# DeltaNet stage of a decoder block: channel weights split in two halves, z copied out of PSUM by ScalarE, the output's turn one chunk later

## The chip, the cores and the metric

One core of a Trainium2 chip. The metric is the device time of the kernel in microseconds, the median of several executions. One execution was also recorded by the hardware profiler; all rows below come from that one.

## What is computed

A decoder block on 1024 tokens of width 1024: an attention branch, a gated DeltaNet branch, a mixture of experts and a per-layer embedding. The change touches the way in which channels of one large input projection are computed, and the DeltaNet branch, which is this (8 heads of width 128):

```python
proj = h @ w_in
qkv_b = silu(causal_short_conv(qkv_b, conv_w))           # q, k, v of each head
beta = sigmoid(beta_b); g = -exp(a_log) * softplus(alpha_b + dt_bias)
a_mat = tril_strict((k * beta) @ k.T * decay)            # inside each chunk
t_mat = inverse(eye + a_mat)                             # unit lower triangular
u, w = t_mat @ (v * beta), t_mat @ (k * beta * exp(gcum))
# over the chunks:
v_new = u - w @ state
o     = (q * exp(gcum)) @ state + attn_intra @ v_new
state = state * exp(g_last) + k_tail.T @ v_new
# at the end:
o_b = rms_norm(o) * silu(z)
```

## The kernel before

Matrix products of the projection are made in fp32r with both operands split: a weight `w` becomes `whi` (a copy rounded to fp32r, by ScalarE, `wsplit` L182) and `wlo = w - whi` (VectorE, L183), and each product is three matmuls (`mm3`, L37 to L39). Engines are called PE (TensorE), ACT (ScalarE), DVE (VectorE), POOL (GpSimd) and SP (which here only issues DMAs).

`channels` (L201) is the projection, one job for 128 channels. A job loads a raw weight of 128x8x128 by a DMA from SP (`wraw`, L173), splits it, and does two halves of 512 tokens, 24 matmuls of 128x512 each, into a PSUM tile `mm` (2 buffers); after each half the job's `done` takes the tile out. The weight of the next job is loaded and split when half 0 is through. There are 2 buffers for `wraw` and 3 for `whi` and `wlo`, so the raw weight of the load after next can be fetched only when both instructions of the present split have read theirs. 42 loads feed the DeltaNet stage (32 of the heads, 10 of gates), 6 more run at the end of the attention stage.

`delta_net` runs the 8 heads as a software pipeline over this feed: one head is one period of 32 feed steps, 4 jobs (k, q, v, z). What a head does between the feed's matmuls is placed by the table `P`: `rows` fetches a row of decays `D` (L711), `decay` makes `eg` and `D` of it (ACT L719 to L724), `job_k`, `job_q`, `job_v` end in a short convolution (ACT L632 and L634, DVE L636 three times, ACT tanh L637, DVE L638), `job_z` in ACT tanh L669 and DVE L671, which reads PSUM, then a DMA `zT` to DRAM (L672). The matrix `nat` (L741) is written to DRAM as `dA` by four DMAs (L751) and comes back spread over 128 partitions as `M` by one DMA (`M<-dA`, L753). `solve` then works on DVE alone: a memset of M's diagonal (L757), and 31 pairs of L764 and L766 with growing width; its result goes through `dT` to `um`. `inverse` joins 32-blocks to the full triangle by small matmuls `px`, `py`, `pyt` (L845 to L868), with copies by ACT and DVE (`xz` L848/L849, `tm` L856, `um` L857/L858, `x` L864).

`scan` is the recurrence over 8 chunks: matmul `pks` (L911), DVE `vb` (L913), matmul `pvn` (L917), ACT `vn` (L920), matmul `po` (L922), matmul `pds` (L930), DVE `S` (L936). After every 4 chunks `out` normalizes: sums `so` (L888, L889), `ro` by DVE L110 and a power on POOL (L111), DVE L891, then ACT `on` (L894, four copies). `turn` transposes `on` on PE (`pot`, L899), multiplies by z on DVE (L900) and stores (`obT`, L902, SP). `late` says how many chunks of the next scan steps lie between `out` and `turn`.

The instruction order on each engine is fixed before the run: a list scheduler goes over the program in the order in which it is written and puts each instruction on its engine by its model of when it is ready, with a priority for the recurrence (`hp`). Each engine, SP too, then works through its list in order and stops at the first instruction whose inputs or buffers are not ready. So an edit that makes more or other instructions can shift others that it does not mention.

Of the kernel before, what the change touches and what calls it, by code (L numbers as in the profile page):

```python
# [11 lines left out]
AF = mybir.ActivationFunctionType  # L12
ALU = mybir.AluOpType
# [18 lines left out]
def r32(ap):  # L32
    return ap.bitcast(F32)


def mm3(nc, out, lh, ll, rh, rl, start, stop):
    nc.tensor.matmul(out, lh, rh, start=start, stop=False)  # L37
    nc.tensor.matmul(out, lh, rl, start=False, stop=False)  # L38
    nc.tensor.matmul(out, ll, rh, start=False, stop=stop)  # L39
# [67 lines left out]
def rstd_pow(k, out, ss, n, eps=EPS):  # L107
    nc = k.nc
    w = out.free_size() if callable(getattr(out, "free_size", None)) else out.shape[-1]
    nc.vector.tensor_scalar(out, ss, 1.0 / n, eps, op0=ALU.mult, op1=ALU.add)  # L110
    return nc.gpsimd.tensor_tensor(out, out, k.mhalf[:, :out.shape[-1]], op=ALU.pow)  # L111
# [57 lines left out]
def wraw(k, srcs, shape=(8, 128), eng=None):  # L169

    raw = k.wpool.tile([128, *shape], F32, name="wraw", tag="wraw", bufs=k.wbufs[0])
    for sl, s in srcs:
        (eng or k.nc.sync).dma_start(raw[sl], s)  # L173
    return raw


def wsplit(k, raw):
    nc = k.nc
    shape = raw.shape[1:]
    hi = k.wpool.tile([128, *shape], F32R, name="whi", tag="whi", bufs=k.wbufs[1])  # L180
    lo = k.wpool.tile([128, *shape], F32R, name="wlo", tag="wlo", bufs=k.wbufs[1])
    nc.scalar.activation(hi, raw, AF.Copy)  # L182
    nc.vector.tensor_tensor(lo, raw, r32(hi), op=ALU.subtract)  # L183
    return hi, lo


def wload(k, srcs, shape=(8, 128), eng=None):
    return wsplit(k, wraw(k, srcs, shape, eng))


def wcols(w, *cols):

    v = w.rearrange("(c p) n -> p c n", p=128)
    out, o = [], 0
    for c0, n in cols:
        out.append(((slice(None), slice(None), slice(o, o + n)), v[:, :, c0:c0 + n]))
        o += n
    return out


def channels(k, jobs):  # L201


    def load(i):
        return wload(k, wcols(k.I["w_in"][0], (jobs[i][0], 128)))

    w = load(0)
    for i, (_, done) in enumerate(jobs):
        for half in range(2):
            p = k.ps_mm.tile([128, 512], F32, name="mm", tag="mm")  # L210
            s = slice(half * 512, half * 512 + 512)
            for c in range(C):
                mm3(k.nc, p, w[0][:, c, :], w[1][:, c, :], k.hh[:, c, s], k.hl[:, c, s], c == 0, c == C - 1)
                if c == C - 1:
                    done(half, p)
                    if half == 0 and i + 1 < len(jobs):
                        then = load(i + 1)
                if c % 2:
                    yield
        w = then if i + 1 < len(jobs) else None  # L220
# [378 lines left out]
def half4(hf):  # L599
    return slice(4 * hf, 4 * hf + 4)  # L600


def cols(x):
    return lambda c: x[:, c * 128:c * 128 + 128]


P = dict(hp=65, every=2, late=(1, 3), tk0=1, tk1=4, rows=0, de0=4, de1=5, kb0=8, kk0=10, kb1=10, kk1=13, solve=15,
         tq0=14, kq0=15, tq1=20, kq1=22, tv0=22, tv1=24, tails=24, turned=37, after=43)


class Head:
# [51 lines left out]
    def job_z(self):  # L663

        k, nc, h = self.k, self.k.nc, self.h

        def done(half, p):
            th = k.thp.tile([128, 512], F32, name="th", bufs=2)
            nc.scalar.activation(th, p, AF.Tanh, scale=0.5)  # L669
            z = k.st.tile([128, 512], F32, name="acc", bufs=2)  # L670
            nc.vector.scalar_tensor_tensor(z, th, 1.0, p, op0=ALU.add, op1=ALU.mult)  # L671
            nc.sync.dma_start(k.zT[h * 128:h * 128 + 128, 512 * half:512 * half + 512], z)  # L672
        return O_QB + 3072 + 128 * h, done

# [148 lines left out]
    def before(self):  # L823
# [8 lines left out]
        for n, g in f.items():  # L832
            slots.setdefault(P[n], []).append(g)
        return slots
# [37 lines left out]
    def scan(self):  # L872

        k, nc, dn, h = self.k, self.k.nc, self.k.dn, self.h
        um = k.um[h % 2]
        hp = lambda: k.tc.high_priority(offset=P["hp"]) if P["hp"] else ExitStack()
        S = None
        late = []

        def out(hf, po):  # L880
            z2 = dn.tile([128, 512], F32, name="z2", bufs=2)
            t4 = slice(512 * hf, 512 * hf + 512)
            nc.sync.dma_start(z2, k.zT[h * 128:h * 128 + 128, t4])
            c4 = half4(hf)
            so = dn.tile([128, 4], F32, name="so", bufs=2)
            self.sumsq(po, so)
            ro = dn.tile([128, 4], F32, name="ro", bufs=2)
            nc.vector.tensor_tensor(so, so, self.rq[:, c4], op=ALU.mult)  # L888
            nc.vector.tensor_tensor(so, so, self.rq[:, c4], op=ALU.mult)  # L889
            rstd_pow(k, ro, so, 128.0)  # L890
            nc.vector.tensor_tensor(ro, ro, self.rq[:, c4], op=ALU.mult)  # L891
            on = dn.tile([128, 4, 128], F32, name="on")
            for i in range(4):
                nc.scalar.activation(on[:, i, :], po[:, i, :], AF.Copy, scale=ro[:, i:i + 1])  # L894

            def turn():
                pt = self.ptile("pot")
                for i in range(4):
                    nc.tensor.transpose(pt[:, i, :], on[:, i, :], k.ident)  # L899
                nc.vector.scalar_tensor_tensor(z2, pt.rearrange("p a b -> p (a b)"), k.dng, z2, op0=ALU.mult,  # L900
                                               op1=ALU.mult)
                nc.sync.dma_start(k.obT[h * 128:h * 128 + 128, t4], z2)  # L902
            late.extend([None] * P["late"][hf] + [turn])

        for c in range(8):
            i = c % 4
            if i == 0:
                po = k.ps_o.tile([128, 4, 128], F32, name="po", tag="o")
            if S is not None:
                ps = k.ps_v.tile([128, 128], F32, name="pks", tag="v")  # L910
                nc.tensor.matmul(ps, cols(self.k2)(c), S, start=True, stop=True)  # L911
                with hp():
                    nc.vector.scalar_tensor_tensor(self.vb[:, c, :], ps, self.co[:, 1, c:c + 1], self.vb[:, c, :],  # L913
                                                   op0=ALU.mult, op1=ALU.add)
# [24 lines left out]
            if i == 3:  # L939
                out(c // 4, po)  # L940
# [472 lines left out]
def expert_split(k, raw):  # L1413
    k.wpool, k.wbufs = k.wgu
    gu = [wsplit(k, r) for r in raw[:4]]
    k.wpool, k.wbufs = k.wdn
    return gu, [wsplit(k, r) for r in raw[4:]]
# [284 lines left out]
def tile_kernel(ctx, tc, I, out):  # L1702
# [25 lines left out]
    with ExitStack() as e0:  # L1728
        with ExitStack() as e1:
# [36 lines left out]
            for i, _ in enumerate(feed):  # L1766
                if i % P["every"] == 0:
                    next(more, None)
# [113 lines left out]
```

## Time and profile before

| | |
|---|---|
| time, median of 3 executions | 2051.33 us (2045.94 to 2053.91) |
| profiled execution | 2063.92 us, span 2062.2 us |
| PE busy | 1962.6 us (95% of the span) |
| PE weight loads | 1672.1 us |
| DVE busy | 1161.1 us (56%) |
| ACT busy | 968.1 us (47%) |
| POOL busy | 195.4 us (9%) |
| mean granted clock of PE | 0.987 |

A busy share is an average over stages: the DeltaNet stage lies from about 580 to 1370 us, its steady heads from 836 to 1240 us with a period of 72 us. An engine whose idle time is named with a releaser was waiting for that instruction or DMA.

### The profile page before, as it was taken

The numbers are of one execution on the slowest core, as the hardware profiler recorded it, in microseconds if no ns is written. First come the engines' busy times: TensorE is split into PE (matmuls) and PEld (weight loads), VectorE is DVE, ScalarE is ACT, GpSimd is POOL, SyncE is SP. The second block draws the span as 40 slices with busy tenths as digits, with TensorE's granted clock in tenths as the row PEclk, the third lists the DMA queues.
The fourth block names the chain that finished last, engine by engine and source line by source line (L and its number), as shares of the span: only waits on it lengthen the run. The fifth ranks groups of instructions, "written<-read, shape, count | busy, mean of one in ns | idle before, by whom it ended". The sixth has DMA issues, their size and how long they took to land.

```text
span 2062.2 us, 35105 instructions
## 1 busy us (share of the span) xinstructions
PE 1962.6 (95%) x13402; PEld 1672.1 (81%) x13402; DVE 1161.1 (56%) x2940; ACT 968.1 (47%) x2573; POOL 195.4 (9%) x196
## 2 busy tenths in 40 slices
PE   7999999999999989999999999979999889999998
PEld 7999999989987777777777777858978767777698
DVE  7253435473422678778877872355474645555655
ACT  6344445444443644565456452232433345555643
POOL 0000000000000001010000100000021244431100
PEclk9999999999999999999999999989999899999999
DMA  4102131242233222232222223585465377776742
GB/s 160 54 28 78 53 105 52 81 138 74 66 110 111 58 67 59 65 85 62 79 76 74 68 68 101 145 246 192 145 204 184 125 238 253 231 246 229 244 157 91
DMA packets 249353, 252.53 MB, mean 122 GB/s; under 512 B 62453, under 2 KB 207142, under 8 KB 248922
## 3 DMA queue, kind: packets, MB, share of 16 engines
q1 hardware_dynamic: 234280, 224.88, 35.8%
q0 software_dynamic: 11776, 24.18, 3.4%
q8 instruction: 107, 1.75, 0.3%
q10 hardware_dynamic: 3122, 1.16, 0.2%
q14 instruction: 68, 0.56, 0.1%
HBM read 202.34 MB, written 64.59 MB: 129 GB/s over the span
## 4 chain that ended last, share of the span: by engine, by line
PE 63%; DVE 14%; DMA 12%; issue 7%; ACT 2%; POOL 1%; SPq 1%; ACTq 0%; DVEq 0%; POOLq 0%
PE mm L37 13%; PE mm L38 13%; PE mm L39 12%; DMA M<-dA 4%; DVE prod L764 3%; DVE tu L766 3%; DMA wraw<-in_w_expert_down_dram 2%; PE gp L37 2%; DVE acc L636 2%; PE gp L39 2%; PE gp L38 1%; PE sc L447 1%; PE pv L475 1%; PE gu L37 1%; PE gu L38 1%
## 5 line engine op out<-in xcount | busy, mean ns | idle before, releaser
L183 DVE TENSOR_TENSOR wlo<-wraw,whi 128x1024 fp32r<-128x1024 f32 x228 | 274.9, 1223 | 213.2 <-ACT whi L182 211.3
L37 PE MATMUL mm<-whi,hTh 128*128 128x256 f32 x1152 | 336.1, 292 | 5.9 <-ACT sqa L406 3.5
L37 PE MATMUL mm<-hTh,whi 128*128 128x512 f32 x768 | 327.0, 426 | 14.7 <-ACT th L962 10.3
L38 PE MATMUL mm<-wlo,hTh 128*128 128x256 f32 x1152 | 327.8, 285 | 0.0
L39 PE MATMUL mm<-whi,hTl 128*128 128x256 f32 x1152 | 327.7, 284 | 0.0
L182 ACT ACTIVATE whi<-wraw 128x1024 fp32r<-128x1024 f32 x228 | 236.0, 1057 | 194.2 <-PE mm L38 113.9
L39 PE MATMUL mm<-hTh,wlo 128*128 128x512 f32 x768 | 304.8, 397 | 0.0
L38 PE MATMUL mm<-hTl,whi 128*128 128x512 f32 x768 | 303.8, 396 | 0.0
L37 PEld LDWEIGHTS mm<-whi,hTh 128*128 128x128 f32 x1152 | 221.8, 193 | 18.0 <-issue 7.3
L38 PEld LDWEIGHTS mm<-wlo,hTh 128*128 128x128 f32 x1152 | 222.1, 193 | 0.8 <-DVE wlo L183 0.7
L39 PEld LDWEIGHTS mm<-whi,hTl 128*128 128x128 f32 x1152 | 221.8, 193 | 0.2 <-DVE rsqx L119 0.2
L37 PEld LDWEIGHTS mm<-hTh,whi 128*128 128x128 f32 x768 | 146.3, 191 | 40.8 <-ACT th L962 10.7
L39 PEld LDWEIGHTS mm<-hTh,wlo 128*128 128x128 f32 x768 | 145.2, 189 | 32.9
L38 PEld LDWEIGHTS mm<-hTl,whi 128*128 128x128 f32 x768 | 146.4, 191 | 22.4
L454 ACT ACTIVATE sm<-sm,nm 128x128 f32<-128x128 f32 (+1 forms) x192 | 84.3, 440 | 87.5 <-DVE nm L452 87.0
L403 ACT ACTIVATE qraw<-mm 128x256 f32<-128x256 f32 x128 | 48.4, 378 | 148.2 <-PE mm L39 148.0
L407 DVE TENSOR_REDUCE ss<-sqa 128x4 f32<-128x256 f32 x96 | 40.1, 418 | 133.0 <-ACT sqa L406 132.9
L636 DVE SCALAR_TENSOR_TENSOR acc<-xp,cols,acc 128x512 f32<-128x512 f32 x144 | 107.7, 748 | 8.1 <-ACT acc L634 5.1
L466 DVE COPY pT<-pt 128x256 f32<-128x256 f32 (+1 forms) x96 | 49.4, 540 | 105.0 <-PE pt L465 105.0
L764 DVE TENSOR_TENSOR prod<-tu,M 128x2 f32<-128x2 f32 (+30 forms) x248 | 83.7, 337 | 6.2
L1520 PE MATMUL gr<-wraw,hr 128*64 128x256 f32 x512 | 67.0, 381 | 9.7 <-ACT hr L1511 9.6
L37 PE MATMUL mm<-whi,mh 128*128 128x256 f32 x256 | 73.6, 289 | 0.1
(402 smaller groups left out, 4077.5 us busy)
## 6 DMA issues: line engine op xcount, KB each, us to landing
wraw<-in_w_in_dram SPq DMA_DIRECT2D x84, 512.0 KB
wraw<-in_w_expert_down_dram SPq DMA_DIRECT2D x30, 512.0 KB
wraw<-in_w_expert_gate_dram SPq DMA_DIRECT2D x60, 256.0 KB
wraw<-in_w_expert_up_dram SPq DMA_DIRECT2D x60, 256.0 KB
gT<-th SPq DMA_DIRECT2D x32, 256.0 KB
wraw<-in_w_branch_b_dram SPq DMA_DIRECT2D x16, 512.0 KB
gate<-gT SPq DMA_DIRECT2D x32, 256.0 KB
wraw<-in_w_out_dram SPq DMA_DIRECT2D x16, 512.0 KB
```

Source lines behind the costliest of these rows:

```text
L37: nc.tensor.matmul(out, lh, rh, start=start, stop=False)
L38: nc.tensor.matmul(out, lh, rl, start=False, stop=False)
L39: nc.tensor.matmul(out, ll, rh, start=False, stop=stop)
L182: nc.scalar.activation(hi, raw, AF.Copy)
L183: nc.vector.tensor_tensor(lo, raw, r32(hi), op=ALU.subtract)
L403: nc.scalar.activation(rows[t], p, AF.Copy)
L454: nc.scalar.activation(x.sm[:, h, :nk], x.sm[:, h, :nk], AF.Exp, bias=nm[:, h:h + 1], accum_out=ml[:, x.t, h, 1:2])
L466: nc.vector.tensor_copy(x.pT[:, 2 * pr:2 * pr + 2, :nk], pt[:, :, :nk])
L636: nc.vector.scalar_tensor_tensor(acc, xp[:, i:i + 512], k.conv(i, b), acc, op0=ALU.mult, op1=ALU.add)
L764: nc.vector.tensor_tensor(pr[:, :j, :n], tu[:, :j, :n], M[:, None, :n, r].to_broadcast([128, j, n]), op=ALU.mult)
L766: nc.vector.tensor_reduce(tu[:, :j, r], pr[:, :j, :n], axis=AX.X, op=ALU.add)
L1520: k.nc.tensor.matmul(self.p[64 * f:64 * f + 64], self.t[:, c, :], w[:, f], start=c == 0, stop=c == 7)
```

## The change

`wsplit` gets a number of parts; `channels` calls it with 2, so each of its weights is split by two copies of 128x512 on ACT and two subtractions of 128x512 on DVE in place of one of 128x1024 each. In `job_z` ACT also copies the PSUM tile into the z tile, and the DVE instruction reads z from there and no longer from PSUM. In `P`, `late` goes from (1, 3) to (2, 4): the output's transposes, their product with z and the store come one chunk later, but for the second half of head 7.

```diff
--- before.py
+++ after.py
@@ -174,13 +174,16 @@
     return raw
 
 
-def wsplit(k, raw):
+def wsplit(k, raw, parts=1):
     nc = k.nc
     shape = raw.shape[1:]
     hi = k.wpool.tile([128, *shape], F32R, name="whi", tag="whi", bufs=k.wbufs[1])
     lo = k.wpool.tile([128, *shape], F32R, name="wlo", tag="wlo", bufs=k.wbufs[1])
-    nc.scalar.activation(hi, raw, AF.Copy)
-    nc.vector.tensor_tensor(lo, raw, r32(hi), op=ALU.subtract)
+    n = shape[0] // parts
+    for i in range(parts):
+        s = slice(n * i, n * i + n)
+        nc.scalar.activation(hi[:, s], raw[:, s], AF.Copy)
+        nc.vector.tensor_tensor(lo[:, s], raw[:, s], r32(hi[:, s]), op=ALU.subtract)
     return hi, lo
 
 
@@ -202,7 +205,7 @@
 
 
     def load(i):
-        return wload(k, wcols(k.I["w_in"][0], (jobs[i][0], 128)))
+        return wsplit(k, wraw(k, wcols(k.I["w_in"][0], (jobs[i][0], 128))), 2)
 
     w = load(0)
     for i, (_, done) in enumerate(jobs):
@@ -604,7 +607,7 @@
     return lambda c: x[:, c * 128:c * 128 + 128]
 
 
-P = dict(hp=65, every=2, late=(1, 3), tk0=1, tk1=4, rows=0, de0=4, de1=5, kb0=8, kk0=10, kb1=10, kk1=13, solve=15,
+P = dict(hp=65, every=2, late=(2, 4), tk0=1, tk1=4, rows=0, de0=4, de1=5, kb0=8, kk0=10, kb1=10, kk1=13, solve=15,
          tq0=14, kq0=15, tq1=20, kq1=22, tv0=22, tv1=24, tails=24, turned=37, after=43)
 
 
@@ -668,7 +671,8 @@
             th = k.thp.tile([128, 512], F32, name="th", bufs=2)
             nc.scalar.activation(th, p, AF.Tanh, scale=0.5)
             z = k.st.tile([128, 512], F32, name="acc", bufs=2)
-            nc.vector.scalar_tensor_tensor(z, th, 1.0, p, op0=ALU.add, op1=ALU.mult)
+            nc.scalar.activation(z, p, AF.Copy)
+            nc.vector.scalar_tensor_tensor(z, th, 1.0, z, op0=ALU.add, op1=ALU.mult)
             nc.sync.dma_start(k.zT[h * 128:h * 128 + 128, 512 * half:512 * half + 512], z)
         return O_QB + 3072 + 128 * h, done
 
@@ -900,7 +904,7 @@
                 nc.vector.scalar_tensor_tensor(z2, pt.rearrange("p a b -> p (a b)"), k.dng, z2, op0=ALU.mult,
                                                op1=ALU.mult)
                 nc.sync.dma_start(k.obT[h * 128:h * 128 + 128, t4], z2)
-            late.extend([None] * P["late"][hf] + [turn])
+            late.extend([None] * (P["late"][hf] - (hf and h == 7)) + [turn])
 
         for c in range(8):
             i = c % 4
```

In the program of the change, lines behind `wsplit` have numbers higher by 3 or 4 (L753 is L757, L757 is L761, L891 is L895, L902 is L906). The order of instructions moves at these places.

SP, in a steady head, from the weight fetch that follows the row of decays `D` to the DMAs after `M<-dA`. Before:

```order
L173 DMA wraw<-in_w_in_dram 128x8x128
L902 DMA obT<-z_10823 128x512
L751 DMA dA<-nat 32x8x32 x4
L883 DMA z_11608<-zT 128x512
L173 DMA wraw<-in_w_in_dram 128x8x128
L753 DMA M<-dA 128x1x1024
L672 DMA zT<-acc 128x512
L173 DMA wraw<-in_w_in_dram 128x8x128
```

And with the change:

```order
L173 DMA wraw<-in_w_in_dram 128x8x128
L755 DMA dA<-nat 32x8x32 x2
L906 DMA obT<-z_10881 128x512
L755 DMA dA<-nat 32x8x32 x2
L887 DMA z_11676<-zT 128x512
L173 DMA wraw<-in_w_in_dram 128x8x128
L757 DMA M<-dA 128x1x1024
L676 DMA zT<-acc 128x512 x2
L173 DMA wraw<-in_w_in_dram 128x8x128
```

The store `obT` has moved between the `dA` DMAs. The fetch `wraw` still stands directly ahead of `M<-dA`.

ACT, in the same head, from the copy `whi` of the split that this `wraw` waits for. Before:

```order
L182 ACTIVATE whi<-wraw 128x1024
L687 ACTIVATE junk,sq<-pq 128x128 x4
L864 ACTIVATE x_11003<-px 64x256
L637 ACTIVATE th<-acc 128x512
L857 ACTIVATE um_7703<-py 32x4x32
L858 ACTIVATE um_7703<-py 32x4x32
L632 ACTIVATE xp<-mm 128x512
L634 ACTIVATE acc<-mm,cols 128x512
L864 ACTIVATE x_11042<-px 64x256
L869 ACTIVATE um_7703<-pyt 64x4x64 x2
```

With the change, from the first half of that split to the second and one row more:

```order
L185 ACTIVATE whi<-wraw 128x512
L635 ACTIVATE xp<-mm 128x512
L640 ACTIVATE th<-acc 128x512
L691 ACTIVATE junk,sq<-pq 128x128 x2
L861 ACTIVATE um_7715<-py 32x4x32
L862 ACTIVATE um_7715<-py 32x4x32
L691 ACTIVATE junk,sq<-pq 128x128 x2
L868 ACTIVATE x_11063<-px 64x256
L637 ACTIVATE acc<-mm,cols 128x512
L868 ACTIVATE x_11102<-px 64x256
L185 ACTIVATE whi<-wraw 128x512
L873 ACTIVATE um_7715<-pyt 64x4x64 x2
```

The second half stands behind both copies `x` (L868, which is L864 before).

DVE, from the split to the memset that waits for M. Before:

```order
L183 TENSOR_TENSOR wlo<-wraw,whi 128x1024
L638 SCALAR_TENSOR_TENSOR v_10104<-th,acc 128x512
L802 TENSOR_TENSOR D<-pkq,D 128x512
L636 SCALAR_TENSOR_TENSOR acc<-xp,cols,acc 128x512
L628 MEMSET xp 128x3
L636 SCALAR_TENSOR_TENSOR acc<-xp,cols,acc 128x512 x2
L638 SCALAR_TENSOR_TENSOR v_10240<-th,acc 128x512
L933 COPY S<-pds 128x128
L671 SCALAR_TENSOR_TENSOR acc<-th,mm 128x512
L757 MEMSET M 128x32
L764 TENSOR_TENSOR prod<-tu,M 128x2
```

With the change:

```order
L641 SCALAR_TENSOR_TENSOR v_10152<-th,acc 128x512
L631 MEMSET xp 128x3
L186 TENSOR_TENSOR wlo<-wraw,whi 128x512
L806 TENSOR_TENSOR D<-pkq,D 128x512
L639 SCALAR_TENSOR_TENSOR acc<-xp,cols,acc 128x512
L186 TENSOR_TENSOR wlo<-wraw,whi 128x512
L639 SCALAR_TENSOR_TENSOR acc<-xp,cols,acc 128x512 x2
L641 SCALAR_TENSOR_TENSOR v_10290<-th,acc 128x512
L937 COPY S<-pds 128x128
L675 SCALAR_TENSOR_TENSOR acc<-th,acc 128x512
L761 MEMSET M 128x32
L810 TENSOR_SCALAR sq<-sq 128x8
```

The second `wlo` half stands behind `D` and one `acc`.

PE, from the transposes `pq` to the second group of `px`, whose result the second `x` copies. Before:

```order
L681 MATMUL pq<-ident,q_10688 128x128 x4
L39 MATMUL mm<-hTh,wlo 128x512
L37 MATMUL mm<-hTh,whi 128x512
L38 MATMUL mm<-hTl,whi 128x512
L862 MATMUL px<-tm,nat 64x64 x4
L39 MATMUL mm<-hTh,wlo 128x512
L37 MATMUL mm<-hTh,whi 128x512
L800 MATMUL pkq<-q_10688,k_10525 128x128 x4
L862 MATMUL px<-tm,nat 64x64 x4
```

With the change:

```order
L685 MATMUL pq<-ident,q_10737 128x128 x4
L38 MATMUL mm<-hTl,whi 128x512
L39 MATMUL mm<-hTh,wlo 128x512
L37 MATMUL mm<-hTh,whi 128x512
L38 MATMUL mm<-hTl,whi 128x512
L866 MATMUL px<-tm,nat 64x64 x4
L39 MATMUL mm<-hTh,wlo 128x512
L37 MATMUL mm<-hTh,whi 128x512
L38 MATMUL mm<-hTl,whi 128x512
L804 MATMUL pkq<-q_10737,k_10579 128x128 x4
L866 MATMUL px<-tm,nat 64x64 x4
```

Five matmuls `mm` stood between `pq` and the second `px`, now seven; over the stretch that begins with the first `py` of this inverse it is 9 before and 13 now.

DVE at the end of a solve, where the first half of the output is normalized. Before:

```order
L936 SCALAR_TENSOR_TENSOR S<-S,t_egl,pds 128x128
L766 TENSOR_REDUCE tu<-prod 128x8
L110 TENSOR_SCALAR ro<-so 128x4
L183 TENSOR_TENSOR wlo<-wraw,whi 128x1024
L913 SCALAR_TENSOR_TENSOR vb<-pks,co,vb 128x128
L891 TENSOR_TENSOR ro<-ro,rq 128x4
L636 SCALAR_TENSOR_TENSOR acc<-xp,cols,acc 128x512 x3
L900 SCALAR_TENSOR_TENSOR z_10560<-pot,dng,z_10560 128x512
```

With the change:

```order
L110 TENSOR_SCALAR ro<-so 128x4
L770 TENSOR_REDUCE tu<-prod 128x8
L940 SCALAR_TENSOR_TENSOR S<-S,t_egl,pds 128x128
L768 TENSOR_TENSOR prod<-tu,M 128x256
L895 TENSOR_TENSOR ro<-ro,rq 128x4
L186 TENSOR_TENSOR wlo<-wraw,whi 128x512
L770 TENSOR_REDUCE tu<-prod 128x8
L917 SCALAR_TENSOR_TENSOR vb<-pks,co,vb 128x128
L639 SCALAR_TENSOR_TENSOR acc<-xp,cols,acc 128x512
L186 TENSOR_TENSOR wlo<-wraw,whi 128x512
```

L891 (now L895) stood behind the weight's subtraction and `vb`; now it stands ahead of both halves.

## Rows read from the trace of the kernel before

**Rows 1.** The page: the chain of work that ended last, share of the span by engine.

```profile
PE 63%; DVE 14%; DMA 12%; issue 7%; ACT 2%; POOL 1%; SPq 1%; ACTq 0%; DVEq 0%; POOLq 0%
```

**Rows 2.** The waits of PE in the steady heads, 836 to 1240 us: who waited for what, us in total, times, longest.

```profile
PE pvn L917 <- DVE vb L913: 9.3, 13, 1.9
PE pks L911 <- DVE S L936: 5.9, 18, 0.5
PE pot L899 <- ACT on L894: 1.2, 5, 0.2
```

**Rows 3.** The same in the first heads, 700 to 836 us.

```profile
PE mm L37 <- DVE acc L671: 4.4, 2, 4.1
PE pk L681 <- DVE k L638: 3.2, 2, 1.8
```

**Rows 4.** Stretches: from:to, length, then busy us (instructions) of PE, PEld, DVE, ACT and POOL, the granted clock of PE, DMA share, GB/s.

```profile
724.00:728.00 4.00, 3.88 (x11) 3.08 (x12) 3.65 (x12) 0.00 (x0) 0.00 (x0) 0.60 0.69 197
778.00:782.00 4.00, 3.56 (x11) 2.98 (x12) 3.69 (x18) 0.00 (x0) 1.64 (x1) 0.57 0.17 66
...
925.00:929.00 4.00, 4.00 (x28) 3.69 (x29) 3.51 (x17) 1.42 (x5) 1.03 (x1) 1.00 0.00 0
```

**Rows 5.** SP's DMA issues in one steady head: start, us of the issue, line, destination and source.

```profile
907.15 0.32 SPq L902 DMA_DIRECT2D obT<-z  x1
910.08 1.82 SPq L751 DMA_DIRECT2D dA<-nat  x4
912.00 0.40 SPq L883 DMA_DIRECT2D z<-zT  x1
912.50 0.40 SPq L173 DMA_DIRECT2D wraw<-in_w_in_dram  x1
913.18 0.56 SPq L753 DMA_DIRECT2D M<-dA  x1
...
934.06 0.39 SPq L173 DMA_DIRECT2D wraw<-in_w_in_dram  x1
```

**Rows 6.** DVE in the same head: start, us, and in brackets the idle time before it with its releaser.

```profile
911.06 0.17 DVE L630 COPY xp<-xp 128x3 f32<-128x3 f32 x1
911.13 1.22 DVE L183 TENSOR_TENSOR wlo<-wraw,whi 128x1024 fp32r<-128x1024 f32 x1
...
923.38 0.09 DVE L757 MEMSET M<- 128x32 f32 x1 [1.97 <-DMA M<-dA]
...
924.55 0.34 DVE L913 SCALAR_TENSOR_TENSOR vb<-pks,co,vb 128x128 f32<-128x128 f32 x1
...
932.82 1.22 DVE L183 TENSOR_TENSOR wlo<-wraw,whi 128x1024 fp32r<-128x1024 f32 x1
...
949.08 0.16 DVE L110 TENSOR_SCALAR ro<-so 128x4 f32<-128x4 f32 x1
...
950.29 0.35 DVE L913 SCALAR_TENSOR_TENSOR vb<-pks,co,vb 128x128 f32<-128x128 f32 x1
951.27 0.16 DVE L891 TENSOR_TENSOR ro<-ro,rq 128x4 f32<-128x4 f32 x1 [0.64 <-POOL ro L111]
```

**Rows 7.** POOL at the end of that solve.

```profile
949.33 1.91 POOL L111 TENSOR_TENSOR ro<-ro,mhalf 128x4 f32<-128x4 f32 x1 [23.29 <-DVE ro L110]
```

**Rows 8.** ACT in the same head: the second copy `x`.

```profile
913.80 0.38 ACT L864 ACTIVATE x<-px 64x256 f32<-64x256 f32 x1
```

**Rows 9.** PE in the same head: the second `px`, and the matmuls around the wait before `pvn`.

```profile
912.41 0.67 PE L862 MATMUL px<-tm,nat 64*64 64x64 f32 x8
...
922.99 0.39 PE L38 MATMUL mm<-hTl,whi 128*128 128x512 f32 x1
923.22 0.40 PE L39 MATMUL mm<-hTh,wlo 128*128 128x512 f32 x1
924.94 0.49 PE L917 MATMUL pvn<-vb,um 128*128 128x128 f32 x2 [1.33 <-DVE vb L913]
```

**Rows 10.** Groups of single lines, 580 to 1372 us: count, least, median and longest duration in ns, first and last start, shape. The halves' own shapes are found in a later line that splits activations in the same way (L991, L992).

```profile
L182 ACT ACTIVATE whi<-wraw x49: 1039/1058/1077, 579.9 to 1367.3; 128x1024 fp32r<-128x1024 f32 x49
...
L183 DVE TENSOR_TENSOR wlo<-wraw,whi x50: 1208/1219/1228, 579.3 to 1368.4; 128x1024 fp32r<-128x1024 f32 x50
...
L991 ACT ACTIVATE obh<-obr x6: 617/630/634, 1359.4 to 1370.1; 128x512 fp32r<-128x512 f32 x6
...
L992 DVE TENSOR_TENSOR obl<-obr,obh x6: 684/693/694, 1360.0 to 1370.7; 128x512 fp32r<-128x512 f32 x6
...
L671 DVE SCALAR_TENSOR_TENSOR acc<-th,mm x16: 673/681/689, 713.5 to 1221.2; 128x512 f32<-128x512 f32 x16
...
L638 DVE SCALAR_TENSOR_TENSOR k<-th,acc x16: 664/692/694, 672.8 to 1170.2; 128x512 f32<-128x512 f32 x16
...
L632 ACT ACTIVATE xp<-mm x48: 573/597/616, 668.4 to 1200.5; 128x512 f32<-128x512 f32 x48
```

**Rows 11.** Head 0, 722 to 735 us: DVE's end of the first z half and of the k job, and the two PE instructions that waited for them.

```profile
723.39 0.67 DVE L671 SCALAR_TENSOR_TENSOR acc<-th,mm 128x512 f32<-128x512 f32 x1
...
733.23 0.68 DVE L638 SCALAR_TENSOR_TENSOR k<-th,acc 128x512 f32<-128x512 f32 x1
...
724.12 0.80 PE L37 MATMUL mm<-hTh,whi 128*128 128x512 f32 x1 [4.11 <-DVE acc L671]
...
734.06 0.63 PE L681 MATMUL pk<-ident,k 128*128 128x128 f32 x4 [1.41 <-DVE k L638]
```

## The prediction

> **What bounds the kernel now.** I read the page first. PE is busy for 95% of the span and holds most of the chain that ended last, DVE and DMA a good part of the rest [rows 1]. The chain alone doesn't say what a change in the DeltaNet stage is worth, so I read next what PE waits for there, since PE's matmuls of the feed fill nearly all of that stage. In the 404 us of the steady heads these waits sum to 16.4 us: 9.3 for `vb`, 5.9 for `S`, 1.2 for `on` [rows 2]. In the first heads 4.4 us go to the wait for DVE to empty PSUM (L671) and 3.2 to `k` (L638) [rows 3]. That is 24 us, the most that any better order of the other engines could give back. What a worse order can cost has no such bound.
>
> The largest single wait of a steady head is one row: `pvn` at 924.94, 1.33 us [rows 9]. Its `vb` ran on DVE at 924.55, behind the memset of M at 923.38, and that memset had waited 1.97 us for the DMA `M<-dA` [rows 6]. DVE was otherwise idle, and `vb` itself needed nothing that late, but DVE goes through its list in order. So the arrival of M is a time to which PE already waits, once in each head: what comes on top of it is added to PE one for one.
>
> When does M come? SP issued it at 913.18, and DVE could use it at 923.38: 10.2 us [rows 5, 6]. What held the issue stands directly ahead in SP's queue: the fetch `wraw` at 912.50, 0.40 us. It may only overwrite a buffer when the split that reads it is done: `wlo` ran at 911.13 for 1.22 us, until 912.35 [rows 6]. A second place reads the same way: `wlo` 932.82 to 934.04, `wraw` issued at 934.06 [rows 5, 6]. From the end of the split to the issue of M it is 0.83 us.
>
> **The split in halves.** Each load gets a second instruction on ACT and on DVE. Halves of the same shape, a copy and a subtraction of 128x512, took 0.630 and 0.693 us, the whole ones 1.058 and 1.219 [rows 10]: 2 x 0.630 - 1.058 = 0.20 us more on ACT, 2 x 0.693 - 1.219 = 0.17 on DVE for each of 42 loads in the stage, 7 us on DVE in all. Most of it falls where DVE is idle, as in the stretches in which it waits for M or for `pot`. Where the solve keeps DVE full, one or two loads a head, the price could reach PE; the bounds are 0 and 2 x 0.17 x 6 = 2 us, and I take 0, because there the first half can also go earlier, between steps of the solve.
>
> [...]
>
> **Where the second half stands.** This is the part that I expect to decide. In the steady head `wraw`, directly ahead of `M<-dA`, now waits for the second half of a split, and this half stands on ACT behind both copies `x` and on DVE behind `D` and one `acc`, where the whole split was done before them. The second `x` needs the second `px` on PE. Step by step: `px` ended at 912.41 + 0.67 = 913.08 [rows 9]. Thirteen `mm` stand ahead of it since the first `py` where nine did; at 0.23 us each, the distance of two starts [rows 9], that is 4 x 0.23 = 0.92: 914.00. Then `x`, 0.38 [rows 8]: 914.38. The second half of `whi`, 0.63: 915.01; of `wlo`, 0.69: 915.70 [rows 10]; then 0.83 to the issue of M: 916.53, which is 3.35 later than 913.18. Neighbouring records overlap a little (`wlo` starts at 911.13, when the row before it, 911.06 + 0.17, has 0.10 to go [rows 6]), so I take off about 0.25 for the chain: **3.1 us later**. From below: if ACT and PE use time that they now spend waiting near the first `py`, so that `px` is late by two matmuls only (-0.46), and the overlaps are 0.2 larger, it is 2.45. From above: if ACT, whose copies have been rearranged in front of it, comes to the second `x` late by two such copies, 0.76, it is 3.9. `obT` between the `dA` DMAs adds its 0.32 and a gap, 0.9 at most with its wait for L900 [rows 5]; it runs beside the chain above and counts only if that chain doesn't hold.
>
> This holds for the six solves of heads 2 to 7; in heads 0 and 1 no such `wraw` is ahead of M. Nothing hides it: DVE's list has `vb` behind M as before, and PE has the same number of `mm` ahead of that `pvn`. The solve behind M moves with it, and with it the later `vb` and `S`; PE moves by the same amount, so they aren't counted twice. 6 x 3.1 = 18.6.
>
> [...]
>
> **L891 ahead of the weight.** Now L891 stands directly behind the last power. POOL took 1.91 us for it at 949.33, to 951.24 [rows 7], and DVE started L891 at 951.27. Between them DVE did 1.22 of split and 0.35 of `vb` and was idle for 0.64 [rows 6]. With the change less lies between L110 and L891: `S` and two solve steps, some 1.2 us, and behind L891 follow half a split and `vb`. `vb` comes later by about the idle time that grows: 0 to 0.5 us, I take +0.4 a head.
>
> **The output's turn.** The wait of `pot` for `on` goes: 1.2 us in 5 of them [rows 2], -0.2 a head; I double it to -0.4 for the small matmuls that are queued behind `pot`, where the wait repeats in part. The z product and `obT` come later, but nothing in the stage reads `obT`, and the z tile has two buffers. So these two parts cancel.
>
> **z by way of SBUF.** ACT gets a copy of 128x512 from PSUM, 0.60 us as L632 [rows 10], 16 times, and has the time. DVE's instruction reads SBUF: L638 does that in 0.692 us, L671 from PSUM takes 0.681 [rows 10]: no gain. PSUM comes free by ACT. In the steady heads PE has no wait for L671 [rows 2]; in head 0 it had 4.1 of the 4.4 us [rows 3, 11], as L671 stood behind a split in the solve (723.39), and the clock granted to PE behind it was 0.60 for 4 us [rows 4], which costs 4 x 0.4 = 1.6. That could be a gain of 5.7 us. But what PE would run earlier soon needs `k`, which DVE made at 733.23 in the same full solve, and PE then already waited 1.41 us for it [rows 11]. DVE's work up to there has become no less, so the wait moves there. Bounds 0 and -6; I take 0.
>
> [...]
>
> **The sum.** 6 x (3.1 + 0.4 - 0.4) = 18.6, less a little for slack that I can't place: +18 us. On the profiled execution that gives 2063.9 + 18 = 2082. That execution was 12.6 us above the median of the runs (2051.33), by more than they spread, with the same program; the sum is a difference, so I put it on the median: **2069 us**.
>
> **The rivals.**
> - *The wait of `wraw` doesn't bind.* If the second half is done early, because PE reaches `px` earlier than I think, M is later only by `obT`, 0.9 at most: 6 x 0.7 = 4 us, 2055. For it: before the change the split ended only 0.15 us ahead of the issue, so a shift of some tenths costs as little. Against it: both x copies stand ahead in ACT's list, and `px` can't come before its matmuls. 0.19.
> - *Faster.* The new order puts `S` and `vb` of the third chunk some 0.6 us earlier against the memset of M, and the turn leaves the full part of DVE. If that takes the waits for `vb` and `S` down by half (-8), `pot` by all of it (-1), and head 0 gives its 5 us, it is -14: 2037. It decides if M's issue doesn't move, so it needs the first rival's condition as well. 0.10.
> - *The stalls drop the clock.* The wait for `pvn` would become 1.3 + 3.1 = 4.4 us. [...] If each of the six does that it is 6 x 1.6 = 10 more: 2079. 0.08, since the stall lies right at the length for which I have few rows.
>
> **How the numbers follow.** Forecast 0.63, its own range 2064 to 2075 (2.45 and 3.9 a head, with a few us of spread of such runs). The range to be held 8 times in 10 takes in the first rival and the clock: 2053 to 2080; it leaves out the faster case and the ends. Half a percent, 10 us, is about what these measurements can tell: slower means above 2062, faster below 2041. Slower: the forecast, but for its lowest tenth, and the clock, 0.67. Same: the first rival and parts of both neighbours, 0.23. Faster 0.10.
>
> **What would show it.** In the trace of the change: `wraw` ahead of M issued at the end of the second `wlo` half, M issued some 3 us later against the `dA` DMAs, the memset's wait for `M<-dA` near 5 us, and PE's `pvn` waiting some 4 us in each of heads 2 to 7, with the group `pvn <- vb` near 9.3 + 18 = 27 us. In head 0 the wait for L671 gone and that for `k` larger by the same. If M's issue keeps its distance to `dA`, the forecast is wrong, and if PE's wait for `vb` shrinks as well, its sign.

## The result, and the profile after

The change makes the kernel slower: 2076.31 us median (2070.02 to 2078.82) against 2052.03 (2045.94 to 2057.95) of the kernel before in the same series; the ratio is 1.0111, with a 95% interval of 1.0087 to 1.0135, or 18 to 28 us. The profiled execution took 2076.84 us.

The page of the profile after: its span, and the chain that ended last (DMA has fallen from 12% to 8%, PE and ACT have risen; [rows 1]).

```profile
span 2075.1 us, 35210 instructions
...
PE 65%; DVE 11%; DMA 8%; issue 8%; ACT 5%; POOL 1%; SPq 1%; ACTq 0%; DVEq 0%; POOLq 0%
```

The waits of PE in the steady heads, 836 to 1240 us, which answer to [rows 2], and then those of 700 to 836 us, which answer to [rows 3].

```profile
PE pvn L921 <- DVE vb L917: 24.8, 11, 4.2
PE pks L915 <- DVE S L940: 1.2, 5, 0.3
PE py L857 <- ACT xz L852: 1.2, 5, 0.2
...
PE pk L685 <- DVE k L641: 7.3, 1, 7.3
```

In the steady heads the wait for `vb` grew from 9.3 to 24.8 us, that for `S` fell from 5.9 to 1.2, and that for `on` is gone. In head 0 the wait for L671 is gone, and `k` is waited for 7.3 us in its place.

SP in the head that answers to [rows 5], in the profile after: start, us, line.

```profile
910.18 0.34 SPq L906 DMA_DIRECT2D obT<-z  x1
910.57 1.58 SPq L755 DMA_DIRECT2D dA<-nat  x2
913.13 0.34 SPq L887 DMA_DIRECT2D z<-zT  x1
915.29 0.40 SPq L173 DMA_DIRECT2D wraw<-in_w_in_dram  x1
915.87 0.56 SPq L757 DMA_DIRECT2D M<-dA  x1
```

DVE around the split that this `wraw` waits for, and on to the recurrence (the memset and `vb` answer to [rows 6]). The first row is the second of the two instructions that make `nat`; the DMAs of `dA` follow it. Below that stand ACT, and PE at the first `pvn` behind M (which answers to [rows 9]).

```profile
908.14 0.69 DVE L745 TENSOR_TENSOR nat<-pkk,D 128x512 f32<-128x512 f32 x1
...
911.12 0.68 DVE L186 TENSOR_TENSOR wlo<-wraw,whi 128x512 fp32r<-128x512 f32 x1
...
914.58 0.69 DVE L186 TENSOR_TENSOR wlo<-wraw,whi 128x512 fp32r<-128x512 f32 x1 [0.32 <-ACT whi L185]
...
925.15 0.13 DVE L810 TENSOR_SCALAR sq<-sq 128x8 f32<-128x8 f32 x1 [4.61 <-issue]
925.17 0.09 DVE L761 MEMSET M<- 128x32 f32 x1
925.55 0.34 DVE L917 SCALAR_TENSOR_TENSOR vb<-pks,co,vb 128x128 f32<-128x128 f32 x1
...
913.51 0.38 ACT L868 ACTIVATE x<-px 64x256 f32<-64x256 f32 x1 [0.47 <-PE px L866]
913.91 0.63 ACT L185 ACTIVATE whi<-wraw 128x512 fp32r<-128x512 f32 x1
...
925.95 0.79 PE L921 MATMUL pvn<-vb,um 128*128 128x128 f32 x2 [3.38 <-DVE vb L917]
```

The chain is the one that the prediction worked through: second `x`, second half of `whi`, of `wlo` (until 915.27), `wraw` at 915.29, `M<-dA` at 915.87. From the second `nat` to the issue of M it is 7.73 us, in each of heads 2 to 7 within 0.01. Before it was 3.8 to 4.2: `nat` at 909.36 in the head shown, issue at 913.18 [rows 5]. M reaches DVE at 925.17, PE waits 3.38 us. DVE's wait for M is the idle time of 4.61 us, near the 5 that I had; it stands at `sq`, behind the memset in the list, whose record starts 0.02 us ahead of it.

Before the change it was not the fetch that held M. The chain of work that ended last, in the profile of the kernel before: start, us, what.

```profile
911.46 1.64 DMA dA<-nat
...
913.18 10.11 DMA M<-dA
```

M was issued when the last `dA` had landed, 0.08 us behind it; the fetch had been issued at 912.50. As means of heads 2 to 7, the last `dA` landed 3.8 us behind the second `nat` before and 4.8 with the change, where `obT` stands between the DMAs of `dA`. So about 1.0 of the 3.8 us by which M's issue moved is this landing, and 2.8 are the wait of the fetch.

The stretches behind that wait in the six heads, columns as in [rows 4]; first the whole of the steady heads.

```profile
836.00:1240.00 404.00, 376.70 (x2408) 308.88 (x2407) 298.68 (x816) 222.94 (x744) 31.51 (x21) 0.95 0.24 70
853.00:857.00 4.00, 4.00 (x18) 3.77 (x18) 3.51 (x17) 1.32 (x5) 0.42 (x1) 0.59 0.00 0
926.00:930.00 4.00, 4.00 (x18) 3.90 (x19) 3.29 (x17) 0.51 (x2) 0.99 (x1) 0.50 0.00 0
1001.00:1005.00 4.00, 3.82 (x17) 3.82 (x18) 3.28 (x18) 0.28 (x1) 1.23 (x1) 0.50 0.01 2
1075.70:1079.70 4.00, 4.00 (x18) 3.90 (x19) 3.28 (x17) 0.52 (x2) 0.98 (x1) 0.50 0.02 4
1150.80:1154.80 4.00, 3.97 (x17) 3.92 (x18) 3.28 (x17) 0.42 (x2) 1.08 (x1) 0.50 0.00 0
1225.70:1229.70 4.00, 3.95 (x17) 3.92 (x18) 3.28 (x17) 0.41 (x2) 1.09 (x1) 0.50 0.02 4
```

Behind each of these waits, of 3.1 to 4.2 us, the granted clock is at 0.50 for the 4 us, in the first head at 0.59: 17 or 18 matmuls where there were 28 [rows 4].

### The profile page after: what moved, and what is told of

Same layout as the page of the kernel before. It is cut to its first block, busy times and chain, and to the rows that moved or that the text cites. A ratio compares the mean times of both kernels' runs of the same rounds, so it can differ in the third digit from the quotient of the medians.

```text
span 2075.1 us, 35210 instructions
## 1 busy us (share of the span) xinstructions
PE 1963.7 (95%) x13402; PEld 1681.0 (81%) x13402; DVE 1163.2 (56%) x2988; ACT 978.8 (47%) x2637; POOL 193.6 (9%) x196
## 4 chain that ended last, share of the span: by engine, by line
PE 65%; DVE 11%; DMA 8%; issue 8%; ACT 5%; POOL 1%; SPq 1%; ACTq 0%; DVEq 0%; POOLq 0%
PE mm L37 14%; PE mm L38 13%; PE mm L39 13%; DVE prod L768 3%; DMA wraw<-in_w_expert_down_dram 2%; DVE tu L770 2%; DVE acc L639 2%; PE gp L37 2%; PE gp L39 1%; PE gp L38 1%; PE sc L450 1%; PE pv L478 1%; PE gu L39 1%; PE gu L37 1%; PE gu L38 1%
## 5 line engine op out<-in xcount | busy, mean ns | idle before, releaser
L186 DVE TENSOR_TENSOR wlo<-wraw,whi 128x1024 fp32r<-128x1024 f32 (+1 forms) x276 | 281.8, 1038 | 223.7 <-ACT whi L185 213.4
L185 ACT ACTIVATE whi<-wraw 128x1024 fp32r<-128x1024 f32 (+1 forms) x276 | 245.7, 910 | 219.0 <-PE mm L38 147.6
```

The costliest lines, as they stand in the source:

```text
L185: nc.scalar.activation(hi[:, s], raw[:, s], AF.Copy)
L186: nc.vector.tensor_tensor(lo[:, s], raw[:, s], r32(hi[:, s]), op=ALU.subtract)
```

## The experiments

All times are medians beside runs of the kernel before on the same chip; the ratios have 95% intervals.

| run | median us | ratio to before |
|---|---|---|
| again (the kernel before) | 2052.69 | 1.0002 (0.9982 to 1.0021) |
| z_only | 2050.16 | 0.9981 (0.9965 to 0.9997) |
| halves | 2064.54 | 1.0056 (1.0033 to 1.0079) |
| late_only | 2063.30 | 1.0046 (1.0028 to 1.0064) |
| z_late | 2065.38 | 1.0056 (1.0039 to 1.0073) |
| halves_z | 2064.03 | 1.0056 (1.0039 to 1.0073) |
| halves_late | 2066.97 | 1.0063 (1.0040 to 1.0085) |
| all_M_on_pool | 2077.10 | 1.0112 (1.0095 to 1.0129) |
| all_vb_first | 2063.36 | 1.0046 (1.0033 to 1.0059) |
| halves_vb_first | 2044.68 | 0.9947 (0.9928 to 0.9966) |
| before_vb_first | 2038.32 | 0.9911 (0.9886 to 0.9937) |
| z_vb_first | 2040.50 | 0.9928 (0.9903 to 0.9953) |

**A second profile of the kernel before.** No edit.

> The kernel before, unchanged, for a second profile. Its first profiled execution took 2063.9 us, 12 above the median of its runs. If that lies in the landing of M (about 10.4 us from issue to use in that profile, 9.5 in the profile of the change), the second profile should be near 2052 with about 9.5 us from issue to use; if the two agree on 10.4, the excess lies elsewhere. The distance from the second nat to the issue of M-from-dA should be 3.8 us again.

Its span is 2051.2 us. From M's issue to its use it took 9.8 us on average in heads 2 to 7, against 10.1 in the first profile, but the seven heads take the same time in both, 499.0 and 499.1 us from the first M to the last. So the landing explains nothing of the 11 us; they all lie behind the last M: from the last memset to the end it is 851.7 us in the first profile, 840.4 in this one. The group of the memset on DVE, with its first and last start, in this profile:

```profile
L757 DVE MEMSET M<- x8: 85/85/85, 711.7 to 1210.8; 128x32 f32 x8
```

And in the profile after:

```profile
L761 DVE MEMSET M<- x8: 85/85/85, 710.1 to 1225.0; 128x32 f32 x8
```

From the first head's M to the last it is 499.1 us before and 514.9 with the change: 15.8 us of the 24 lie in these seven periods. PE's waits in the steady stretch of this second profile sum to 14.5 us, those after to 27.2: 12.7 more. Over exactly the five periods between the M of head 2 and the M of head 7, all its waits take 12.4 us more, of 15.3 us.

**Each part alone.** The change with the two other parts undone. The first three lines say in short what is undone in each run; the edit below them undoes the copy of z, in `halves` and `late_only`.

```diff
# halves:    late=(1, 3), z from PSUM
# z_only:    wsplit in one part, late=(1, 3)
# late_only: wsplit in one part, z from PSUM
-            nc.scalar.activation(z, p, AF.Copy)
-            nc.vector.scalar_tensor_tensor(z, th, 1.0, z, op0=ALU.add, op1=ALU.mult)
+            nc.vector.scalar_tensor_tensor(z, th, 1.0, p, op0=ALU.add, op1=ALU.mult)
```

> Only the split in halves; late stays (1, 3), z is read from PSUM. In this order M's DMA stands ahead of the weight fetch in SP's list and no longer behind it. Theory (the issue of M decides): M issued 3 us or less behind the second nat, PE's wait for vb below the 9.3 us of before, 2042 to 2052 us. Rival (the halves cost by themselves, 0.17 us on DVE for each of 42 loads, in the part where DVE is full): 2056 to 2060 us, wherever M is.

> Only z copied by ACT. Theory: the weight fetch stays ahead of M's DMA but waits for a whole split as before, distance 3.8 us, so no change: 2048 to 2056. In head 0 the wait for L671 gone and that for k larger by as much. Rival (PSUM's release is worth what head 0 waited): 2046 or less by 5 us.

> Only late (2, 4). In this order M's DMA stands ahead of the weight fetch, the store obT between the dA DMAs. Theory (the issue of M decides): 2042 to 2053 us, PE's wait for vb not above before. Rival (the later turn costs by itself, by obT ahead of M and by pot in another place): 2060 us or more, with the distance from nat to M's issue above 4.5 us.

z alone did as expected, down to head 0, where the wait for `k` rose to 8.0 us as that for L671 went. The halves alone and the later turn alone were slower by 10 and 9 us, though in both M's DMA stood ahead of the weight fetch. Both expectations missed. The time of the halves lies above the rival's range too; the later turn has the rival's time. What PE waits for in the steady heads with the halves alone:

```profile
PE pks L914 <- DVE S L936: 8.3, 6, 2.6
PE pvn L920 <- DVE vb L916: 7.2, 17, 1.0
```

And with the later turn alone:

```profile
PE pks L914 <- DVE S L936: 10.7, 6, 3.2
PE pvn L920 <- DVE vb L916: 9.6, 16, 0.7
```

The first line of each is new. L936 is the copied `S` of the first chunk (L933 before). DVE in the run of the halves:

```profile
994.34 0.25 DVE L936 COPY S<-pds 128x128 f32<-128x128 f32 x1 [4.59 <-PE mm L39]
994.36 0.09 DVE L760 MEMSET M<- 128x32 f32 x1
```

The copy runs together with the memset, once M is there: in these orders DVE's list has the memset ahead of `S`, as the orders of `before` and z_only don't. Its input, the matmul `pds`, had run on PE at 991.12 already. So an earlier step of the recurrence was queued behind M.

With the halves alone M was hardly later: issued 3.85 us behind the second `nat` in four heads, 4.23 and 5.61 in the other two. The expected 3 us or less could not come, since the last `dA` landed no earlier than 3.7. With the later turn alone M was itself later, 5.0 to 6.9 us behind `nat`, above the 4.5 that the rival had named, and without any fetch ahead of it. SP in one head of this run, where the second `nat` starts at 900.62:

```profile
903.16 0.34 SPq L905 DMA_DIRECT2D obT<-z  x1
903.55 0.96 SPq L754 DMA_DIRECT2D dA<-nat  x2
...
905.86 0.56 SPq L756 DMA_DIRECT2D M<-dA  x1
```

`obT` stands between the DMAs of `dA`, and M is issued when the last of them has landed. That last one is issued 3.4 us behind `nat` here, where it was 2.1 before; in two of the heads it also took 3.4 us to land, where it took 1.64 or 1.65 in the six heads of the kernel before. So with the later turn M is 1.2 us late and more, before any fetch stands ahead of it.

**Two parts at a time, and M on another queue.** Each leaves out one part of the change; the fourth has all three, and

```diff
-        nc.sync.dma_start(M.rearrange("p a b -> p (a b)"), dA[None, :, :].to_broadcast([4, 32, 1024]))
+        nc.gpsimd.dma_start(M.rearrange("p a b -> p (a b)"), dA[None, :, :].to_broadcast([4, 32, 1024]))
```

> The change without the halves (z and late). M's DMA stands ahead of the weight fetch. Theory (the issue of M behind the second half decides): 2042 to 2053 us, distance from the second nat to M's issue 4.5 us or less, no drop of the clock behind pvn. Rival (late costs by itself): 2060 or more.

> The change without the later turn. M's DMA stands ahead of the weight fetch. Theory: 2042 to 2053 us, distance 3 us or less. Rival (the halves are what costs): 2060 us or more.

> The change without the copy of z. The weight fetch stands directly ahead of M's DMA and waits for the second half. Theory: as slow as the whole change, 2070 to 2080 us, distance 7.7 us, PE's wait for vb some 25 us, clock at 0.5 behind it. Rival (z's copy on ACT is what delays the second half): 2060 or less and a distance near 5 us.

> The whole change, with M's DMA issued from POOL's queue in place of SP's, so that the weight fetch is not ahead of it; the rest of the order moves only a little. Theory: M issued as soon as dA has landed, 3 to 4.5 us behind the second nat, at most 1 us more for the issue on POOL; PE's wait for vb back to 10 us or less and no drop of the clock: 2040 to 2054. Rival (the halves or the later turn cost by themselves): stays above 2062.

z_late and halves_z are again the case of `S` behind the memset: 13.1 and 8.6 us of waits for it. Both expectations missed, in time and in distance: M is issued 5.1 to 7.3 us behind `nat` in z_late and 3.9 to 5.1 in halves_z, and in two heads of z_late the clock fell to 0.50. halves_late is the case of the whole change: distance 7.7 us, wait for `vb` 24.9, mean clock 0.96. But its time is 2067, below what I expected, and 10 us below the whole change, though its profile shows the same mechanism. In its seven heads it takes 512.3 us, against 514.9; 2.6 of the 10 us are there. Most of the rest lies behind the last M, from where it is 841.4 us to the end against 850.1; the reason stays open.

With M on POOL nothing was gained, and the expectation missed: M is issued 5.1 to 6.5 us behind `nat`, not 3 to 4.5. In one head:

```profile
912.70 0.69 DVE L745 TENSOR_TENSOR nat<-pkk,D 128x512 f32<-128x512 f32 x1
...
929.82 0.09 DVE L761 MEMSET M<- 128x32 f32 x1 [4.72 <-DMA M<-dA]
...
918.55 0.74 POOL L757 DMA_DIRECT2D M<-dA  x1 [16.82 <-DMA dA<-nat]
...
931.19 0.80 PE L921 MATMUL pvn<-vb,um 128*128 128x128 f32 x2 [4.05 <-DVE tu L770]
```

M is issued 5.85 us behind `nat`, 1.9 earlier than in the change, but it lands 11.3 us after that and not 9.3: the memset comes 17.1 us behind `nat`, as before this edit. The run didn't take the delay away, so it tells nothing against it, nor for it. POOL too waited for `dA`, the releaser in its row: without the fetch ahead of it M can go no earlier than that.

**What stands behind the memset.** The memset is ordered behind the `vb` of the second chunk, and three steps later in the program, in the change, in the halves alone, in the kernel before and in z_only:

```diff
-        nc.vector.memset(M.rearrange("p a b -> p (a b)")[:, 0::33], 1.0)
+        yield
+        yield
+        yield
+        with k.tc.issue_after(k.last_vb) if getattr(k, 'last_vb', None) else ExitStack():
+            nc.vector.memset(M.rearrange("p a b -> p (a b)")[:, 0::33], 1.0)
...
-                    nc.vector.scalar_tensor_tensor(self.vb[:, c, :], ps, self.co[:, 1, c:c + 1], self.vb[:, c, :],
-                                                   op0=ALU.mult, op1=ALU.add)
+                    k.last_vb = nc.vector.scalar_tensor_tensor(self.vb[:, c, :], ps, self.co[:, 1, c:c + 1], self.vb[:, c, :],
+                                                   op0=ALU.mult, op1=ALU.add).ins
```

> Only the halves, with the same ordering of the memset behind vb. Theory (the 11 us that the halves cost alone are the wait for S, which that order puts behind the memset): PE's wait of 8 us for the copied S gone, 2044 to 2056 us. Rival (the halves' own 7 us of DVE time): 2058 to 2064.

The 8.3 us for the copied `S` are gone and the time falls by 20 us, from 2064.5 to 2044.7, faster than the kernel before. But the same ordering speeds up the kernel before as well, by 17 us (next run). Beside that run the halves still cost some 6 us, so the wait for `S` is only a part of the 10 us that they cost alone.

> The kernel before with the same ordering. Theory: the wait for vb of 7 to 9 us in the steady heads falls by at least 5: 2042 to 2050 us. Rival (DVE is full from M on, so a solve that can start no earlier pushes the later vb): no change, 2050 to 2055, with the wait moved to later chunks.

> Only z copied by ACT, with the same ordering: 3 us below the kernel before with that ordering if the two effects add (z alone was at 0.9981 of before), 2040 to 2048 us; equal to it if z alone was noise.

Both are faster than the kernel before, by 0.9 and 0.7%; they don't differ from each other, so z's copy brought nothing measurable here. The time of before_vb_first is even below the expected range. DVE in one head of the first:

```profile
915.81 0.35 DVE L917 SCALAR_TENSOR_TENSOR vb<-pks,co,vb 128x128 f32<-128x128 f32 x1 [0.27 <-PE pks L915]
916.19 0.09 DVE L761 MEMSET M<- 128x32 f32 x1
```

Its waits of PE in the steady heads:

```profile
PE pvn L921 <- DVE vb L917: 6.6, 12, 0.8
...
PE pks L915 <- DVE S L940: 0.7, 3, 0.2
```

And that stretch, columns as in [rows 4]:

```profile
836.00:1240.00 404.00, 394.99 (x2573) 320.62 (x2572) 313.36 (x834) 225.02 (x737) 32.52 (x23) 1.00 0.28 78
```

With M issued some 4 us behind `nat`, the memset directly behind `vb` waits for M at most 0.5 us, and no wait of PE for `vb` is longer than 0.8 us. The sum of these waits did not fall by the 5 us expected, only from 9.3 or 7.4 to 6.6; what fell is the wait for `S`, from 5.9 to 0.7. The whole gain lies in the heads (482.4 us from the first M to the last, against 499.1), but the waits in the steady stretch fall by only 6.5 us, from 14.5 to 8.0; the rest stays open.

> The whole change, with one thing more: DVE's memset that waits for M is ordered behind the second chunk's vb of the recurrence, so that neither S nor that vb stands behind it. M is issued as late as in the change (7.7 us behind the second nat). Theory (what M's arrival costs is what is queued behind the memset on DVE): the 25 us that PE waits for vb fall below 8, the clock stays at 1.00 in the steady heads, 2045 to 2058 us. Rival (the solve's later end, or the halves and the turn by themselves): 2066 or more though the wait is gone.

Here M is as late as in the change. The wait for `vb` went from 24.8 to 4.9 us, as the theory says, and the time fell by some 13 us; but it ended between the two forecasts, and the clock didn't stay at 1.00 in five of the six heads, as shown below. The waits of PE in the steady heads:

```profile
PE pks L919 <- DVE S L944: 19.0, 8, 3.4
PE pvn L925 <- DVE vb L921: 4.9, 11, 0.8
```

DVE and PE in one head of this run:

```profile
920.38 0.35 DVE L921 SCALAR_TENSOR_TENSOR vb<-pks,co,vb 128x128 f32<-128x128 f32 x1 [0.17 <-PE pks L919]
...
924.18 0.09 DVE L765 MEMSET M<- 128x32 f32 x1 [3.44 <-DMA M<-dA]
...
929.14 0.34 DVE L944 SCALAR_TENSOR_TENSOR S<-S,t_egl,pds 128x128 f32<-128x128 f32 x1
...
929.54 0.49 PE L919 MATMUL pks<-S,k 128*128 128x128 f32 x2 [2.80 <-DVE S L944]
```

M comes 3.44 us after DVE has reached the memset, and the next step of the recurrence, `S`, now stands behind the memset and the solve's first steps: the wait has moved one place on. This wait too is followed by the lower clock, in five of the six heads. One of them, columns as in [rows 4]:

```profile
1003.50:1006.70 3.20, 3.20 (x11) 2.73 (x10) 3.06 (x11) 1.63 (x6) 0.00 (x0) 0.50 0.06 21
```

Beside before_vb_first this run is the nearest comparison: in both the memset stands directly behind that `vb` on DVE, M is issued 3.7 us earlier or later on average, and the times are 2038 and 2063 us. Of these 25 us, 18 are the wait for `S` in the steady stretch (0.7 and 19.0). The two runs differ in the three parts of the change as well, and the halves have a cost of their own, some 6 us in the pair above; so not all of the 25 us can be put down to M.

## Why the prediction was right, point by point

**The mechanism.** The fetch `wraw` ahead of M waits for the second half of a split; M comes later, `vb` waits behind the memset, PE waits for `vb`. Each link stands in the rows above. That the order behind the memset matters is shown by an edit (all_vb_first against the change); that M's lateness does is shown in every head of the traces, but no run moved M alone. The time is inside the range, 7 us above the forecast of 2069 and 1 us above the forecast's own range, 2064 to 2075; the ratio's interval, 18 to 28 us, begins at my +18. The seven periods take 15.8 us more, which is near the sum; the 8 us on top, outside them, had no term in it, and the range reached that far only for the sake of the clock.

**What held M.** I read the fetch as what held M's issue before the change. The rows above say otherwise: it was the landing of `dA`, and my 0.83 us from the end of the split to the issue was not the price of the fetch; with the change it is 0.60. For `obT` I allowed 0.9 at most, and only if the other chain fails; in the change it is about 1.0, in late_only 1.2 and more. In the change the fetch was the later of the two, so the forecast held.

**The size of the delay.** I forecast 3.1 us, bounds 2.45 and 3.9. Against `nat` it is 7.73 - 3.8 = 3.9, the upper bound. To see what reaches PE, I count from the `pvn` of the head before. For the head shown these are, before and after:

```profile
852.93 0.49 PE L917 MATMUL pvn<-vb,um 128*128 128x128 f32 x2 [1.65 <-DVE vb L913]
...
852.38 0.49 PE L921 MATMUL pvn<-vb,um 128*128 128x128 f32 x2 [3.08 <-DVE vb L917]
```

Here the issue is 3.24 us later (63.49 against 60.25), between the 3.35 of the steps and the 3.1 that I took. As means of heads 3 to 7:

| us behind the `pvn` of the head before | before | with the change |
|---|---|---|
| second `nat` | 56.4 | 56.5 |
| issue of M | 60.3 | 64.3 |
| memset of M | 70.2 | 73.9 |
| `pvn` | 71.8 | 74.7 |

The issue is 4.0 us later, just above my upper bound, but `pvn` only 2.9 (3.0 against the second profile). So it was not added one for one, as I had it: M took 0.3 us less from issue to use, and `vb` now stands nearer to the memset, 0.38 us behind it in the head shown and not 1.17 [rows 6], which gives 0.8 back. Both terms I had at nothing, and their sum made up for what the issue came later: 2.9 is near my 3.1 by luck. The wait before `pvn` grew by 3.38 - 1.33 = 2.05 us in the head shown, and the group from 9.3, or 7.4 in the second profile, to 24.8. My figure of 27 was for the same group.

**The clock.** I gave the drop 0.08, as a rival with its own price of 1.6 us a head. It happened in all six heads, at waits of 3.1 to 4.2 us, shorter than the 4.4 for which I had worked it out. This step failed as a chance; the trace of the kernel before had already shown a drop behind a wait of 3.15 us (`pks` at 778.44), to 0.57 over 4 us, in the second of the two stretches of [rows 4], and I had read only the one of 4.1. As a price it was too high. I had worked out the 1.6 from the one stretch at 0.60 in head 0 [rows 4]; the heads take 15.8 us more and the waits explain 12.7, so that only some 3 us show, about half a microsecond a head, of what the lower clock takes from PE. From a late `pvn` to the next second `nat` it is 56.5 us with the lower clock and 56.4 without (table above), so the loss is made up within the head. While the clock is low, DVE, with the solve, is busy for 3.3 to 3.5 of the 4 us (stretches above), and I take it that PE would have waited for `S` and `vb` there, since the wait for `S` fell from 5.9 to 1.2 us. That this is all that makes it up is argued, not shown.

**The halves at nothing.** I took 0 for their own instructions, upper bound 2. halves_vb_first against before_vb_first, ratios 0.9947 and 0.9911, makes it some 6 us; the intervals overlap by a little, but every run of the one (2042.4 to 2046.2) is longer than every run of the other (2035.2 to 2039.0). The durations were right, 0.631 and 0.686 us as medians of the halves in the profile after; the cover was not, as PE waited there, in the steady heads of halves_vb_first, 3.7 us for `nat`.

**L891.** `vb` at the end of the solve came 27.4 us after the memset and not 26.9, as I had it; but POOL took 1.01 us this time and DVE had no idle time, so the reason was the work in front, not the wait. The number was right by luck.

**Head 0, z, and the turn.** The wait for L671 moved to `k`, 7.3 us; L671 with SBUF input took 0.688 us, the copy 0.592. As forecast, worth nothing. The wait of `pot` went.

**What I didn't see.** My reading held for the whole change but not for its parts: I expected the halves, the turn and both with z to be harmless, and each cost 0.5%. In all four `S` waited behind the same memset; with the turn M was later as well, by `obT`, and the halves have some 6 us of their own. The forecast of the change rested on its printed order; the parts' orders had to be read at the memset too, and I had looked at SP alone, and there only at the fetch.

**What stays open.** Of the 24 us some 8 lie outside the seven periods, and the kernel before varied by 11 us there from one profile to the next; and why halves_late is 10 us faster than the whole change is not explained by its heads. No run has the change's order with M's issue early, so the price of the late issue by itself is read from the traces only.

## What to carry to other kernels

Here the wait of one DMA in SP's queue delayed what was queued behind it: the fetch was issued at 915.29, 0.02 us behind the end of the split, M at 915.87, and of the 3.8 us by which M's issue moved 2.8 are that wait. So before splitting an instruction into parts, look up which DMA waits for the last part, and which transfer stands behind that DMA. Look up as well what the transfer itself waits for: that the fetch stood directly ahead of M didn't make it the one that held M. On the consumer, look at what is queued behind the first instruction that needs the transfer: here one step of the recurrence moved ahead of it was worth 0.9%, more than every part of the change cost alone. When a run of one part contradicts the theory, read the order at the consumer before giving the cost to the part itself.

## What the runs showed of the hardware that was not expected

The granted clock fell to 0.50 (0.59 over the 4 us in the first head) behind idle stretches of PE of 3.1 to 4.2 us, in all six heads of the change. The length of the one wait doesn't settle it: in all_vb_first the clock fell (0.50 in the stretch shown above) around waits of 2.88, 2.90, 3.39, 3.33 and 3.02 us, and stayed at 1.00 from 924 to 934 us around one of 2.80 (mean of its steady heads 0.98); with the halves alone it fell behind waits of 2.55 and 2.08 (mean of its steady heads 0.99), and with the later turn alone it stayed at 1.00 from 1066 to 1072 us behind one of 3.10. The same broadcast DMA of M took 9.3 us from issue to use from SP's queue and 11.3 from POOL's in the heads shown, 9.5 and 11.1 as means of heads 2 to 7. Whether the queue makes the difference is not shown: from SP the fetch was issued just ahead of M, from POOL just behind it.
